# Products of the identity in gaps of TensorE: any free bank of PSUM in place of 128 columns at the end of the pair of banks

## The chip, the cores and the metric

One program runs on one core of a Trainium2 chip. The metric is device time in microseconds (us) of one execution, the median of three runs. Durations are read from one further execution that the hardware profiler recorded. Engines are named as the profile names them: PE is TensorE (matmuls) and PEld its weight loads, DVE is VectorE, ACT is ScalarE, POOL is GpSimd, SP is SyncE, which issues the DMAs.

## The reference

The reference is a two-layer diffusion backbone over 512 latent tokens and 256 context tokens of width 1024, all in float32. Each layer is a half-step SwiGLU, a token mixer and a second half-step SwiGLU, and each of them ends in a LayerNorm of `alpha * x + gate * f(x * (1 + scale) + shift)`, where gate, scale and shift come from a conditioning vector. The mixer of layer 0 is a bidirectional gated DeltaNet with four heads beside a Conformer module with a 31-tap depthwise convolution over 512 channels; that of layer 1 is grouped-query attention, eight query heads on two key heads, with normalised and rotated queries and keys.

```python
def ffn_sublayer(x, shift, scale, gate, w_gu, w_down, g, b):
    y = swiglu(modulate(x, shift, scale), w_gu, w_down)
    return deepnorm_residual(x, MACARON_WEIGHT * gate * y, g, b)

def even_mixer(...):    # layer 0: DeltaNet || Conformer, then one output projection
    o_l, _, _ = gdn_bidirectional(*lat_in, s_f, s_b)
    lat_out = merge(o_l, z_l, glu_l)
```

Nothing of this is computed by the instructions that the change touches.

## The kernel before

The kernel is first recorded and then ordered. `Program.record` notes every operation with the tiles that it reads and writes. `Program.order` then walks through a modelled time: whenever an engine is free, it takes the ready operation with the lowest rank that finds room for its tiles, and it writes one list of instructions for all engines. `Program.emit` turns this list into instructions, and semaphores between engines are set by the tile framework below it. So each engine runs its own queue strictly in the order that was planned, and all emitted instructions carry one line, 516 (517 in the changed kernel).

PSUM has eight banks of 512 float32 columns. Six of them are single places, tag `b`. The other two are one place, tag `bb`: one tile `pair` of 1024 columns, of which a tile of tag `bb` has the first 896. Only the convolution `conv31` asks for `bb`, for an accumulator of 783 columns that DVE updates tap by tap; when it is free, an ordinary tile of 512 columns may lie there too.

Where TensorE has nothing to do in the plan, `order` puts in a product of the identity with itself, 128x128, whose result nobody reads (lines 387 to 406). Each is a copy of one recorded matmul, `self.keep`; it stands in the list at the planned time, and none is added while enough of the planned time just before is work (`KEEP`). In the kernel before all of them write into columns 896 to 1023 of `pair`, one tile for the whole program, whatever else lies in the pair. A float32 matmul shows as two rows in the trace, so one product of the identity is two rows `pair<-ident`.

```python
if t.tag == "bb" or t is self.keep.tiles[0]:
    if pair is None:
        pair = p.tile([128, 1024], F32, name="pair")
    t.made = pair[:, 0:t.shape[1]] if t.tag else pair[:, 896:1024]
    continue
```

A tile with a tag gets a slot (`t.slot`), and `p.tile(..., tag=f"{tag}_{slot}", bufs=1)` makes it anew in that slot. Its first writer then waits for every instruction that used the tile which had the slot before; this is how a matmul that begins a new accumulation waits for the copy out of the old one.

Of the kernel before, what the change touches and what calls it, by code (L numbers as in the profile page):

```python
# [10 lines left out]
F32 = mybir.dt.float32  # L11
# [18 lines left out]
class View:  # L30
# [30 lines left out]
    def real(self):  # L61
        v = self.tile.made
        for f, a, k in self.how:
            v = getattr(v, f)(*a, **k)
        return v
# [26 lines left out]


CLASSES = {"p2": 512, "p4": 1024, "p6": 1536}
BANKS = {"b": 512, "bb": 896}


class Op:
# [19 lines left out]
class Program:  # L118
# [113 lines left out]
    def classes(self, occ):  # L232

        used = [t for t in self.tiles if t.tag and t.first is not None]
        for t in used:
            t.epoch = None
            if t.tag not in CLASSES:
                occ[t.tag][t.first:t.last + 1] += 1
            if t.tag in BANKS:
                t.places = [(c, None, n > BANKS[t.tag]) for c, n in BANKS.items() if n >= BANKS[t.tag] and self.slots[c]]  # L240
        ends = [b for b, _, _ in self.epochs[1:]] + [len(self.ops)]
# [23 lines left out]
    def order(self, look=40.0, reserve=1, ahead=40.0):  # L265
        ops = self.ops
        N = len(ops) - (self.keep is not None)
        if self.keep:
            ops.pop()
            self.keep.n = self.keep.deps[0]  # L270
            for t in self.keep.tiles:
                t.left -= 1
        users = [[] for _ in range(N)]
        for o in ops:
            o.wait, o.est, o.start = len(o.deps), 0.0, None
# [8 lines left out]
        occ, free = {}, {}  # L284
# [23 lines left out]
        wire, table, frontier, done = 0.0, 0, 0, 0  # L308
# [4 lines left out]
        now = 0.0  # L313
# [6 lines left out]
        def place(t, sync):  # L320

            for c, e, _ in sorted(t.places, key=lambda x: (x[2] > 0, x[0] != t.tag)) if t.places else ((t.tag, None, 0),):
                if e is not None and (e < self.now or any(left[:e])) or not free[c] or free[c][0][0] > now:
                    continue
                a = min(frontier, t.first)
                keep = reserve if sync and t.pool == "work" and t.places else 0
                if c != t.tag:
                    if occ[c][a:t.last + 1].max() + keep >= self.slots[c]:
                        continue
                elif t.first != frontier and a < t.first and occ[c][a:t.first].max() + keep >= self.slots[c]:  # L330
                    continue
                return c, e
            return None
# [11 lines left out]
        while done < N:  # L345
            moved = False
            for e in engines:
# [8 lines left out]
                while r and tries < 100:  # L356
                    c = heapq.heappop(r)
                    o = ops[c[1]]
# [23 lines left out]
                if pick is None and frontier < N:  # L382
                    o = ops[frontier]
                    if o.eng == e and not o.wait and o.est <= now and fits(o):
                        pick = (o.pri, o.n)
                if pick is None:
                    if e == "tensor" and self.keep and ops[self.keep.n].start is not None and ops[self.keep.n].end < now and 0 < frontier:
                        recent = [x for x in recent if x[1] > now - self.WINDOW]
                        if sum(y - max(x, now - self.WINDOW) for x, y in recent) < KEEP * self.WINDOW:
                            moved = True  # L390
                            o = Op()
                            for x in Op.__slots__:
                                setattr(o, x, getattr(self.keep, x, None))
                            o.n, o.deps, o.tiles, o.bytes = len(ops), [], self.keep.tiles, 0
                            ops.append(o)
                            while now >= edge:
                                warm = busy > 0.75 * self.WINDOW or warm and busy > 0.33 * self.WINDOW
                                busy, edge = 0.0, edge + self.WINDOW
                            cost = o.cost * (1 if warm else 2)
                            busy += cost  # L400
                            o.start, o.at, o.end = now, len(seq), now + cost
                            seq.append(o)
                            idle[e] = o.end
                            recent.append((now, o.end))
                        else:
                            again = now + 0.1
                    continue
                o = ops[pick[1]]
# [8 lines left out]
                for t in o.tiles:  # L417
                    if t.tag and t.slot is None:
                        c, e2 = place(t, o.eng == "sync")
# [59 lines left out]
            if not moved:  # L479
# [7 lines left out]
                now = min(nxt)  # L487
# [4 lines left out]
    def emit(self, tc, pools, seq):  # L492
        nc = tc.nc
        real = lambda v: v.real() if isinstance(v, View) else v
        self.names = {}
        now = part = pair = None
        with tc.manual_schedule():
            for o in seq:
                for t in o.tiles:
                    if t.made is None:  # L500
                        k = {"tag": f"{t.tag}_{t.slot}", "bufs": 1} if t.tag else {}
                        p = pools[t.pool]
                        if t.tag == "bb" or t is self.keep.tiles[0]:
                            if pair is None:
                                pair = p.tile([128, 1024], F32, name="pair")
                            t.made = pair[:, 0:t.shape[1]] if t.tag else pair[:, 896:1024]
                            continue
                        if t.epoch is not None:
                            if now != t.epoch:
                                if now is not None:  # L510
                                    part.release()
                                now, part = t.epoch, tc.alloc_tile_pool(name=f"part{t.epoch}", bufs=1, reuse_waits="tile")
                            p = part
                        t.made = p.tile(t.shape, t.dt, name=t.name, **k)
                f = getattr(getattr(nc, o.eng), o.f)
                i = f(*[real(x) for x in o.a], **{k: real(x) for k, x in o.k.items()})  # L516
                self.names[o.n] = i.ins.name
            if now is not None:
                part.release()
# [145 lines left out]
class Net:  # L665
# [7 lines left out]
        return self.nc.tile([128, 512], F32, "b", "psum", "b")  # L673

    def banks(self):
        return self.nc.tile([128, 896], F32, "bb", "psum", "bb")

    def page(self, dt=F32):
        return self.nc.tile([128, 1024], dt, "p4", "work", "p4")
# [1491 lines left out]
```

## Time and profile before

| | |
|---|---|
| median of 3 runs | 2856.68 us (2853.25 to 2857.43) |
| the profiled execution | 2857.14 us |
| its span in the trace | 2855.4 us |
| PE busy | 2811.3 us, 98% of the span |
| products of the identity | 748 rows, 103.4 us busy |
| granted TensorE clock, mean | 0.992 of 2.4 GHz |

The span runs from the first instruction of the program to the last, and the execution's own time is 1.74 us longer. A busy time is the union of the rows of an engine. Matmuls overlap in their pipeline, so two rows of 0.28 us that start 0.11 us apart take 0.11 us each from the engine's time. The granted clock has two levels here, 1.00 (2.4 GHz) and 0.50 (1.2 GHz).

### The profile page before, as it was taken

The page shows a single profiled execution, that of the slowest core. Times are in us where ns is not written, and L with a number is a line of the kernel's source. Part 1 is how long each engine was busy: PE and PEld are TensorE (multiplying, and loading weights), DVE is VectorE, ACT ScalarE, POOL GpSimd, SP SyncE. Part 2 cuts the span into 40 slices and gives each one's busy share as a digit, 9 for nine tenths or more (in the row PEclk, how much of TensorE's full clock was granted, in tenths as well). Part 3 has the DMA queues.
Part 4 walks back from the last instruction along what each step waited for, and adds up shares of the span by engine and source line. Part 5 has one row for each costly group of instructions (what it writes and reads, how often), then busy time and mean ns, then how long its engine had stood idle before and what let it go on. Part 6 is the DMA issues. An engine that isn't in the chain of part 4 may idle for free. (4 is left out here: it accounts for less than half of the span.)

```text
span 2855.4 us, 48739 instructions
## 1 busy us (share of the span) xinstructions
PE 2811.3 (98%) x19533; PEld 2675.8 (94%) x19533; DVE 2059.9 (72%) x3510; ACT 1136.8 (40%) x1990; POOL 475.4 (17%) x582
## 2 busy tenths in 40 slices
PE   9999999999999899999999999999999999999999
PEld 7999999988778899999999999999999887899998
DVE  3687777677968887787867678766656767788854
ACT  4343332154334744434322145443223555455522
POOL 3000000042865704000000030000003432200001
PEclk9999999999999999999999999999999999999999
DMA  7443465234631132343465225444621221144541
GB/s 243 132 141 115 140 210 181 83 97 137 162 91 44 53 114 88 117 131 124 133 201 188 82 82 170 128 131 155 218 80 31 78 70 48 47 135 143 173 120 46
DMA packets 386016, 346.98 MB, mean 122 GB/s; under 512 B 38528, under 2 KB 338813, under 8 KB 385789
## 3 DMA queue, kind: packets, MB, share of 16 engines
q1 hardware_dynamic: 385789, 343.86, 38.6%
q8 instruction: 154, 2.52, 0.4%
q14 instruction: 73, 0.60, 0.1%
HBM read 296.33 MB, written 47.48 MB: 120 GB/s over the span
## 5 line engine op out<-in xcount | busy, mean ns | idle before, releaser
L516 PE MATMUL b<-p,p 128*128 128x384 f32 (+4 forms) x15711 | 2463.3, 316 | 14.1 <-DVE p L516 6.6
L516 PEld LDWEIGHTS b<-p,p 128*128 128x128 f32 (+1 forms) x15711 | 2341.3, 189 | 86.9 <-issue 17.3
L516 ACT ACTIVATE p<-p 128x1024 fp32r<-128x1024 f32 (+9 forms) x871 | 696.3, 824 | 1093.8 <-PE b L516 410.6
L516 DVE TENSOR_TENSOR p<-p,p 128x1024 fp32r<-128x1024 f32 (+7 forms) x922 | 850.9, 943 | 263.4 <-PE b L516 135.7
L516 ACT ACTIVATE p<-b 128x384 f32<-128x384 f32 (+8 forms) x556 | 250.0, 464 | 485.6 <-PE b L516 445.5
L516 DVE TENSOR_TENSOR p<-p,b 128x384 f32<-128x384 f32 (+3 forms) x396 | 222.5, 578 | 99.0 <-PE b L516 64.0
L516 DVE SCALAR_TENSOR_TENSOR p<-b,gate,p 128x256 f32<-128x256 f32 (+1 forms) x415 | 167.5, 434 | 159.9 <-PE b L516 157.4
L516 POOL TENSOR_TENSOR p<-p,p 128x1024 fp32r<-128x1024 f32 (+18 forms) x157 | 139.1, 888 | 844.7 <-PE b L516 466.3
L516 POOL TENSOR_SCALAR p<-p,cA,cB 128x256 f32<-128x256 f32 x56 | 35.9, 645 | 1241.1 <-DVE p L516 1178.1
L516 DVE SCALAR_TENSOR_TENSOR p<-p,cond,p 128x1024 f32<-128x1024 f32 x161 | 203.0, 1278 | 9.9 <-DMA p<-in_ada_w_dram 9.8
L516 DVE SCALAR_TENSOR_TENSOR pair<-p,dw,pair 128x783 f32<-128x783 f32 x116 | 120.2, 1036 | 6.1 <-PE pair L516 3.4
L516 PE MATMUL pair<-ident 128*128 128x128 f32 x748 | 103.4, 284 | 9.2 <-DVE pair L516 3.7
L516 ACT ACTIVATE p<-p,cB,cA 128x256 f32<-128x256 f32 (+1 forms) x168 | 84.3, 589 | 65.4 <-DVE p L516 65.4
L516 PEld LDWEIGHTS pair<-ident 128*128 128x128 f32 x748 | 93.6, 196 | 16.2 <-ACT p L516 4.7
L516 POOL TENSOR_SCALAR p<-p,lnag 128x256 f32<-128x256 f32 x112 | 96.3, 869 | 3.2 <-DVE p L516 2.9
L516 DVE TENSOR_TENSOR p<-b,p 128x128 f32<-128x128 f32 (+4 forms) x168 | 70.0, 451 | 36.1 <-ACT p L516 18.9
L516 PE MATMUL pair<-p,p 128*128 128x256 f32 (+3 forms) x505 | 90.5, 314 | 0.1
L516 PE MATMUL b<-ident,p 128*128 128x128 f32 (+2 forms) x495 | 78.1, 282 | 3.4 <-DVE p L516 1.2
L516 PEld LDWEIGHTS pair<-p,p 128*128 128x128 f32 x505 | 75.8, 188 | 5.0 <-issue 1.4
L516 DVE TENSOR_TENSOR p<-p 128x512 f32<-128x512 f32 (+1 forms) x90 | 59.9, 674 | 26.0 <-PE b L516 18.5
L516 PEld LDWEIGHTS b<-ident,p 128*128 128x128 f32 (+2 forms) x495 | 59.4, 151 | 20.5 <-issue 7.8
L516 DVE SCALAR_TENSOR_TENSOR p<-p,p 128x384 f32<-128x384 f32 (+2 forms) x104 | 54.3, 534 | 9.2 <-ACT p L516 8.5
(162 smaller groups left out, 1152.8 us busy)
## 6 DMA issues: line engine op xcount, KB each, us to landing
p<-in_ffn_w_gu_dram SPq DMA_DIRECT2D x176, 512.0 KB
p<-in_ada_w_dram SPq DMA_DIRECT2D x144, 512.0 KB
p<-in_ffn_w_down_dram SPq DMA_DIRECT2D x96, 384.0 KB
hd<-p SPq DMA_DIRECT2D x54, 384.0 KB
p<-hd SPq DMA_DIRECT2D x27, 768.0 KB
p<-in_even_w_in_dram SPq DMA_DIRECT2D x25, 512.0 KB
xd<-p SPq DMA_DIRECT2D x24, 512.0 KB
p<-xd SPq DMA_DIRECT2D x24, 512.0 KB
```

The costliest lines, as they stand in the source:

```text
L516: i = f(*[real(x) for x in o.a], **{k: real(x) for k, x in o.k.items()})
```

## The change

The tile `bb` becomes the whole pair. A product of the identity now takes, at its planned time, a free place, `bb` first and then one of the `b`; it makes a new tile in that slot and gives the slot back at once. Where no place is free in the plan, no product is put in. The shared columns 896 to 1023 are gone.

```diff
-BANKS = {"b": 512, "bb": 896}
+BANKS = {"b": 512, "bb": 1024}
...
             for t in self.keep.tiles:
                 t.left -= 1
+            self.keep.tiles = self.keep.tiles[1:]
...
                 if pick is None:
-                    if e == "tensor" and self.keep and ops[self.keep.n].start is not None and ops[self.keep.n].end < now and 0 < frontier:
+                    place1 = next((c for c in ("bb", "b") if free[c] and free[c][0][0] < now), None) if e == "tensor" and self.keep else None
+                    if place1 and ops[self.keep.n].start is not None and ops[self.keep.n].end < now:
...
-                            o.n, o.deps, o.tiles, o.bytes = len(ops), [], self.keep.tiles, 0
+                            v = self.tile([128, 512], F32, "b", "psum", place1)
+                            v.tile.slot = heapq.heappop(free[place1])[1]
+                            o.n, o.deps, o.tiles, o.bytes = len(ops), [], [v.tile] + self.keep.tiles, 0
+                            o.a = (v[:, 0:128],) + self.keep.a[1:]
                             ops.append(o)
...
                             recent.append((now, o.end))
+                            heapq.heappush(free[place1], (now, v.tile.slot))
...
-                        if t.tag == "bb" or t is self.keep.tiles[0]:
-                            if pair is None:
-                                pair = p.tile([128, 1024], F32, name="pair")
-                            t.made = pair[:, 0:t.shape[1]] if t.tag else pair[:, 896:1024]
-                            continue
...
-        return self.nc.tile([128, 896], F32, "bb", "psum", "bb")
+        return self.nc.tile([128, 1024], F32, "bb", "psum", "bb")
```

The order of the instructions shows what comes of it. There are 374 products before and 243 after; the 17346 other matmuls are the same, and 13654 of them stand at the same place among themselves. What stands in brackets names the engine whose semaphore the instruction waits for.

The first place is PE's queue in the projections of layer 0, before the first matmul of the gates (`b_771`). It was:

```order
L516 MATMUL pair_88<-p6_662_5407,p4_806_5648 128x512
L516 MATMUL pair_88<-p6_666_5440,p4_806_5648 128x512
L516 MATMUL pair_88<-p6_662_5407,p4_807_5771 128x512
L516 MATMUL pair_88<-ident_2_70 128x128 [waits Activation_49]
L516 MATMUL pair_88<-ident_2_70 128x128 x28
L516 MATMUL b_771_6133<-gt_766_6128,cum0_749_5141 128x24 [waits DVE_49,Pool_49]
L516 MATMUL pair_88<-ident_2_70 128x128 x3
```

There are as many products now, each a new tile; these are the last of the 29 and the work behind them:

```order
L517 MATMUL b_3937_6196<-ident_2_70 128x128 [waits PE_49]
L517 MATMUL b_3938_6201<-ident_2_70 128x128 [waits PE_49]
L517 MATMUL b_3939_6203<-ident_2_70 128x128 [waits PE_49]
L517 MATMUL b_771_6206<-gt_766_6199,cum0_749_5164 128x24 [waits DVE_49,Pool_49]
L517 MATMUL b_3940_6208<-ident_2_70 128x128 [waits PE_49]
L517 MATMUL b_3941_6214<-ident_2_70 128x128 [waits PE_49]
L517 MATMUL b_3942_6216<-ident_2_70 128x128 [waits PE_49]
L517 MATMUL b_771_6206<-gt_766_6199,cum1_750_5196 128x24 [waits DVE_49,Pool_49]
```

Each product but the first now waits for PE's own semaphore, at the value that the product in the row above it sets; before, none of the 28 waited.

The second place is the end of PE's queue, behind the last matmul of the last layer (`b_3847`). It was:

```order
L516 MATMUL b_3847_28194<-p4_3822_28138,p4_3809_27682 128x512
L516 MATMUL b_3847_28194<-p4_3821_28130,p4_3810_27696 128x512
L516 MATMUL pair_88<-ident_2_70 128x128 x11
L516 MATMUL pair_88<-ident_2_70 128x128 [waits Activation_49]
L516 MATMUL pair_88<-ident_2_70 128x128 x44
L2165 UNCONDITIONAL_BRANCH
```

Of the 55 products that stand there now, these are the 10th to the 16th:

```order
L517 MATMUL b_4048_28362<-ident_2_70 128x128 [waits PE_49]
L517 MATMUL b_4049_28366<-ident_2_70 128x128 [waits PE_49]
L517 MATMUL b_4050_28370<-ident_2_70 128x128 [waits Activation_49]
L517 MATMUL b_4051_28373<-ident_2_70 128x128 [waits PE_49]
L517 MATMUL b_4052_28378<-ident_2_70 128x128 [waits PE_49]
L517 MATMUL b_4053_28381<-ident_2_70 128x128 [waits PE_49]
L517 MATMUL b_4054_28385<-ident_2_70 128x128 [waits PE_49]
```

The first eleven go round five banks, each waiting for the one five rows above or for ACT's copy; the twelfth waits for ACT's copy out of the pair, as before; the 43 behind it all use the pair, each waiting for the one above.

The third place is attention, where PE stood before with:

```order
L516 MATMUL pair_88<-ident_2_70 128x128 [waits DVE_49]
L516 MATMUL pair_88<-ident_2_70 128x128 x9
L516 MATMUL b_2883_21612<-p4_2761_21343,p4_2825_21374 128x256 [waits DVE_49,PE_49,Activation_49]
L516 MATMUL b_2883_21612<-p4_2762_21353,p4_2825_21374 128x256
L516 MATMUL b_2883_21612<-p4_2761_21343,p4_2826_21392 128x256
L516 MATMUL pair_88<-ident_2_70 128x128 x2
```

and has now:

```order
L517 MATMUL b_2878_21699<-p4_2874_21385,p6_2684_20769 128x256
L517 MATMUL b_2883_21758<-p4_2761_21498,p4_2825_21529 128x256 [waits DVE_49,PE_49,Activation_49]
L517 MATMUL b_2883_21758<-p4_2762_21508,p4_2825_21529 128x256
L517 MATMUL b_2883_21758<-p4_2761_21498,p4_2826_21547 128x256
L517 MATMUL b_2882_21766<-ident_2_70,p4_2880_21744 128x128 [waits DVE_49,Activation_49]
```

No place in PSUM is free in the plan there, and all 67 products of this stage are gone.

## Rows read from the trace of the kernel before

**Rows 1.** The page: span, busy time and instructions of each engine, granted clock in 40 slices.
```profile
span 2855.4 us, 48739 instructions
PE 2811.3 (98%) x19533; PEld 2675.8 (94%) x19533; DVE 2059.9 (72%) x3510; ACT 1136.8 (40%) x1990; POOL 475.4 (17%) x582
...
PEclk9999999999999999999999999999999999999999
```
**Rows 2.** The page's groups: out<-in, form, xcount | busy us, mean ns | idle before, releaser.
```profile
L516 PE MATMUL pair<-ident 128*128 128x128 f32 x748 | 103.4, 284 | 9.2 <-DVE pair L516 3.7
```
**Rows 3.** Timeline of PE from 650 us: start, duration, instructions [idle before <-releaser].
```profile
651.01 6.74 PE L516 MATMUL pair<-ident 128*128 128x128 f32 x58 [0.69 <-ACT p L516]
657.59 0.30 PE L516 MATMUL b<-gt,cum 128*128 128x24 f32 x2
657.73 0.91 PE L516 MATMUL pair<-ident 128*128 128x128 f32 x6
658.48 0.30 PE L516 MATMUL b<-gt,cum 128*128 128x24 f32 x2
```
**Rows 4.** Timeline of all engines at the end of the program.
```profile
2838.78 0.19 ACT L516 ACTIVATION_READ_ACCUMULATOR p<-pair 128x1 f32 x1
...
2839.03 10.31 PE L516 MATMUL pair<-ident 128*128 128x128 f32 x90 [0.78 <-ACT p L516]
...
2850.63 1.21 DVE L516 TENSOR_TENSOR p<-p,p 128x1024 f32<-128x1024 f32 x1
```
**Rows 5.** Timeline of PE: products at the cold start, and one alone at 951 us.
```profile
1.64 2.08 PE L516 MATMUL pair<-ident 128*128 128x128 f32 x8 [1.64 <-POOL ident L516]
...
3.86 1.22 PE L516 MATMUL pair<-ident 128*128 128x128 f32 x4
...
951.32 0.49 PE L516 MATMUL pair<-ident 128*128 128x128 f32 x2 [1.13 <-DVE pair L516]
```
**Rows 6.** Stretches of PE: length, busy (x rows), granted clock, DMA share, GB/s.
```profile
819.50:822.28 2.78, 0.25 (x2) 1.00 0.30 50
822.28:829.10 6.82, 6.82 (x22) 0.50 0.77 145
...
944.60:951.98 7.38, 4.93 (x41) 1.00 0.00 0
951.98:955.39 3.41, 3.41 (x25) 0.50 0.43 149
...
2250.00:2470.00 220.00, 212.68 (x1454) 1.00 0.21 63
```
**Rows 7.** Timeline of PE: two more long runs, and what follows them.
```profile
23.79 3.96 PE L516 MATMUL pair<-ident 128*128 128x128 f32 x34
27.55 0.74 PE L516 MATMUL b<-p,p 128*128 128x256 f32 x4
...
31.04 0.59 PE L516 MATMUL b<-p,cond 128*32 128x256 f32 x2 [1.25 <-DMA p<-in_ada_w_dram]
...
1107.54 5.40 PE L516 MATMUL pair<-ident 128*128 128x128 f32 x46
1113.64 0.74 PE L516 MATMUL b<-p,p 128*128 128x256 f32 x4 [0.71 <-ACT p L516]
```
**Rows 8.** Waits of PE: who waited for whom, us in total, times, longest.
```profile
PE pair L516 <- DVE pair L516: 3.7, 4, 1.3
```
**Rows 9.** Instructions on the tile pair: the taps, duration in ns min/median/max.
```profile
L516 DVE SCALAR_TENSOR_TENSOR pair<-p,dw,pair x116: 1023/1039/1041, 695.0 to 972.7; 128x783 f32<-128x783 f32 x116
```
**Rows 10.** Timeline of PE before the last stage's matmuls.
```profile
2819.60 3.07 PE L516 MATMUL pair<-ident 128*128 128x128 f32 x26
...
2822.77 1.67 PE L516 MATMUL b<-p,p 128*128 128x512 f32 x6
```

More of the change, by code (lines that the diff above doesn't have):

```diff
@@ L495, in emit @@
         self.names = {}
-        now = part = pair = None
+        now = part = None
         with tc.manual_schedule():
```

## Prediction

> **What bounds the kernel now.** I read the page first. PE is busy 98% of the span and idles 44 us in all [rows 1], so the kernel is bound by PE's queue: what delays the queue delays the end, save where one of these few idles can swallow it. The granted clock is near 1.00 in every slice, so PE also works at full speed. Then I read the groups: the products of the identity are 748 rows, 374 products, and take 103 us of PE [rows 2]. They lie where the plan has nothing else. The timelines of PE show how well they fit: the run of 29 from 651.01 us ends as the gap ends, and the matmul of the gates follows at once at 657.59 [rows 3]; likewise the runs from 23.79 and 1107.54 [rows 7]. A run that grew longer would push the work behind it. The last view is the end of the program: PE's last 45 products run from 2839.03 to 2849.34, while DVE's last instruction ends at 2851.84 [rows 4]. There PE is the earlier of the two by 2.5 us, and the span ends at 2855.4.
>
> **What a product costs before.** 90 rows take 10.31 us [rows 4], and one product alone takes 0.49 us from its start to its end [rows 5]. So each of the other 44 adds (10.31 - 0.49) / 44 = 0.223 us: they overlap in the pipeline, because none waits for another. At the cold start two products take 1.22 us and four 2.08 [rows 5]: 0.43 us for one more, 1.22 - 0.43 = 0.79 for one alone.
>
> **What a product costs after.** Every product is a new tile in a slot whose last user was most often the product just before it. I counted in the order: of 243 products 224 wait for PE's own semaphore, and 197 of these wait for the product directly ahead. No product before did so. A waiting product can't overlap: it starts after the other's end. No row shows an instruction of PE that waits for the one just ahead, so the price is bounded. From below it is 0.223 us, if the semaphore were seen at issue. From above it is the length of one alone and the step from a releaser's end to PE's start, which is 2838.97 to 2839.03, or 0.06 us [rows 4]: 0.49 + 0.06 = 0.55 us. I take the upper end, since that is how PE stands behind any other engine. At the low clock it is 0.79 + 0.06 = 0.85 us. So a waiting product costs 0.33 us more, and 0.63 us more where the clock has fallen.
>
> **Does the clock fall?** Between 944.60 and 951.98 PE runs products that stand apart by waits; the granted clock is 1.00 there and 0.50 in the 3.41 us behind it. An empty stretch of 2.8 us to 822.28 is followed by 6.8 us at 0.50 [rows 6]. Runs of waiting products look like the first of these: short idles between products, for longer. I take it that a run keeps the high clock for about as long as that stretch did, 7.2 us or 13 products, and then goes on at 0.85 us each.
>
> The Trainium skill, "TensorE: Matmul & The Clock Gate", section "A second HAM failure mode: psum-queue depth-cycling", says that a PE which goes round its PSUM banks and idles a little between groups makes its clock drop and return, and pays for it between the bursts. The trace agrees at the one place just told. With this rule the sum below is 67 us, without it 40 us.
>
> **The sum, against the profiled execution's 2857.1 us** (its span is 1.7 us shorter; it stands 0.4 us above the median of the runs).
>
> Long runs. With 13 products at 0.55, the others at 0.85 and the last at 0.43 before the next matmul can start:
> - 17 products at 23.79: 7.15 + 3 x 0.85 + 0.43 = 10.1 us where the gap was 3.76 [rows 7], so 6.4 more; of this the wait for a DMA at 31.04 can hide 1.25 [rows 7]. Left: +5.1.
> - 29 at 651.01: 7.15 + 15 x 0.85 + 0.43 = 20.3 against 6.58 [rows 3]: +13.7. Behind it stands the gates' chain through DVE, which nothing overlaps.
> - 24 at 1107.54 (23 before): 16.1 against 6.10 [rows 7]: +10.0.
> - The end: ACT's copy releases the pair at 2838.97 as before, then 44 products take 7.15 + 30 x 0.85 + 0.79 = 33.4, to 2872.5. The program's closing costs from 0 to 3.6 us (the latter is 2851.84 to 2855.4, with the last transfer in it); without a transfer I take 0.7. So 2873.2 for 2855.4: +17.8. What was hidden behind DVE by 2.5 us is then the last thing that ends.
>
> The four are 46.6 us; at the high clock throughout they are 4.0 + 9.0 + 6.8 + 8.5 = 28.3.
>
> Short runs. 197 - (16 + 28 + 23 + 43) = 87 waiting products are left; 6 lie ahead of the first transfers and 22 around 930 us. 59 x 0.33 = +19.5. Their gaps are full as well, as in [rows 3] at 657.73, where the next matmul follows in the row behind.
>
> The end of the DeltaNet stage, 927 to 955 us: 35 products at 0.223 and 3.7 us of waits for DVE's taps, which hold the pair [rows 8], give way to 25 products at 0.55 that wait for no tap: 13.8 - 11.5 = +2.3. The taps themselves gain nothing from a bank of their own, they take 1023 to 1041 ns whatever runs beside them [rows 9].
>
> Products that go. In attention 67 x 0.223 = 15 us of PE, in a stretch of which PE is busy 212.7 of 220 us [rows 6]. Where a product held work that was ready this is a gain, where PE would have waited it is none: 0 to -15; I take -6, since in my reading of that timeline PE still idles behind nearly half of the runs. Elsewhere 19 more go: 0 to -4, take -2. Where they leave PE empty the clock may fall, at 3.4 to 6.8 us of half speed [rows 6], or 1.7 to 3.4 us each: two such falls, +4. At 2819.60 thirteen products go and PE is empty for 3.2 us until 2822.77 [rows 10], longer than before the fall at 822.28: +2.5.
>
> After each of the three long runs within the program the clock stays low for at least 3.4 us of full work [rows 6]: 3 x 1.7 = +5.
>
> Together 46.6 + 19.5 + 2.3 - 6 - 2 + 4 + 2.5 + 5 = 72. Of PE's 44 idle us in the span some lie behind these places and wait for something that is not delayed; I take 5 off: **+67, so 2924 us**.
>
> **Rivals.**
> - The clock holds. For it: rows 6 have a single fall after spaced products, and that stretch held waits of up to 1.13 us [rows 5], longer than the 0.33 here. Then 28.3 + 19.5 + 2.3 - 6 - 2 + 2.5 - 5 = 40: 2897 us. The section of the skill named above speaks against it.
> - The runs inside are swallowed, and only the end counts: if the work behind a gap is later than the trace makes it look, because the stage's end hangs on DVE or POOL. For it: DVE is busy 72% [rows 1], and conv taps and scan run beside PE. Against it: the matmuls behind the long runs follow within 0.71 us [rows 3, 7]. Then +8.5 to +17.8, about 2870 us.
> - Faster: PE doesn't really wait for itself, since a matmul's semaphore would be up by the time the next is issued. Then a product costs 0.223 us as before, there are 131 fewer, and the 3.7 us of waits for the taps [rows 8] go too: -6 - 2 - 4 = -12, 2845 us. It decides below about 0.25 us from product to product. Against it: the pipeline overlaps rows of 0.28 us [rows 2], and the end of a row, not its start, is what has released every waiter in these views.
>
> **How the numbers follow.** The fall of the clock 0.62; the clock holds 0.24; only the end 0.08; faster 0.06, of which a third could shrink into no change. A measurement of this kernel can tell 0.2%, 5.7 us, from no change. So slower 0.94, same 0.02, faster 0.04. The likeliest case alone, with 0.55 to 0.9 us at the low clock and none or 15 us of gain in attention, reaches from 2905 to 2950; with the case of the held clock and its own spread the range is 2880 to 2950, and what lies outside it is the last two cases and the tails of the first, 2 in 10.
>
> **What would show it.** Products in the run from 651 us about 0.55 us apart, later 0.85, and the matmul of the gates some 14 us later behind it; the granted clock at 0.50 inside that run and inside the one before the end; PE's last product ending behind DVE's last instruction, by 10 to 20 us; fewer products' rows than before, about 486, but more PE time per product. It is wrong if products stand 0.22 us apart, if the span ends with DVE as before, or if the gates start as early after 651 us as they did.

## The result, and the profile after

The changed kernel takes 2900.09 us (2895.02 to 2902.49) where the kernel before takes 2856.68: a ratio of 1.0152, 95% interval 1.0127 to 1.0177, slower by 43 us. Its profiled execution is 2895.02 us long, 37.9 us more than that of before. The forecast was 2924, and the rival "the clock holds" 2897.

The page of the changed kernel, against [rows 1]:

```profile
span 2893.1 us, 48210 instructions
PE 2837.3 (98%) x19271; PEld 2660.3 (92%) x19271; DVE 2059.0 (71%) x3510; ACT 1135.5 (39%) x1988; POOL 478.7 (17%) x582
...
PEclk9999999899999999999999999999999999999999
```

PE is busy 26.0 us longer with 262 rows fewer, and idles 55.8 us in place of 44.1. The other engines do what they did. PEclk falls below 0.9 nowhere but in one slice, from 506 to 579 us.

The group of the products, against [rows 2]:

```profile
L517 PE MATMUL b<-ident 128*128 128x128 f32 x486 | 116.6, 326 | 14.9 <-POOL ident L517 1.6 <-ACT p L517 0.9 <-DVE p L517 0.8
```

There are 243 products for 374, and yet 116.6 us for 103.4. The long runs in PE's timeline (start, duration, instructions), against [rows 3] and [rows 7]:

```profile
21.47 9.13 PE L517 MATMUL b<-ident 128*128 128x128 f32 x34
30.36 0.72 PE L517 MATMUL b<-p,p 128*128 128x256 f32 x4
...
657.40 15.79 PE L517 MATMUL b<-ident 128*128 128x128 f32 x58 [0.69 <-ACT p L517]
673.03 0.30 PE L517 MATMUL b<-gt,cum 128*128 128x24 f32 x2
673.25 1.58 PE L517 MATMUL b<-ident 128*128 128x128 f32 x6
674.67 0.30 PE L517 MATMUL b<-gt,cum 128*128 128x24 f32 x2
...
1128.47 13.06 PE L517 MATMUL b<-ident 128*128 128x128 f32 x48
1141.29 0.72 PE L517 MATMUL b<-p,p 128*128 128x256 f32 x4
```

The same 29 products take 15.63 us from the first to the matmul of the gates, where they took 6.58; the next matmul still follows at once. The granted clock inside this run, by stretches (length, PE busy, PEld busy, DVE, ACT, POOL, clock, DMA share, GB/s):

```profile
657.40:660.80 3.40, 3.05 (x13) 1.90 (x14) 3.40 (x9) 1.03 (x3) 0.00 (x0) 1.00 0.00 0
...
667.60:671.00 3.40, 3.05 (x14) 1.78 (x12) 0.00 (x0) 0.00 (x0) 0.00 (x0) 1.00 0.00 0
```

It is 1.00 from end to end, where the forecast had 0.50 from the 14th product on. So it is in the run of 24 and in the one behind the last matmul (length, PE busy, clock, DMA share, GB/s):

```profile
1128.47:1141.29 12.82, 11.48 (x52) 1.00 0.63 205
2866.00:2892.34 26.34, 23.83 (x111) 1.00 0.20 80
```

Here the forecast failed. The end of the program, all engines, against [rows 4]; the weight loads show the spacing of the products:

```profile
2880.78 1.21 DVE L517 TENSOR_TENSOR p<-p,p 128x1024 f32<-128x1024 f32 x1
...
2891.31 0.30 PEld L517 LDWEIGHTS b<-ident 128*128 128x128 f32 x2 [0.25 <-PE b L517]
2891.85 0.30 PEld L517 LDWEIGHTS b<-ident 128*128 128x128 f32 x2 [0.25 <-PE b L517]
```

```profile
2866.00 26.34 PE L517 MATMUL b<-ident 128*128 128x128 f32 x110
```

Each product of these rows is released by PE itself (`<-PE b`), 0.547 us after the one before. DVE is done at 2881.99, PE at 2892.34: the last thing that ends is now a product whose result nobody reads.

**Where the 37.7 us of span lie.** I matched the matmuls that both traces have and took the difference of their starts, as a median over 25 us of the time before:

| time before, us | shift at the end of it | what changed in it |
|---|---|---|
| to 200 | -0.3 | -2.3 ahead of the run of 17, +2.0 behind it, given back between 100 and 200 |
| 550 to 575 | +4.1 | +4.4: a fall of the clock that before did not have |
| 600 to 650 | +6.4 | +2.3: the run of 8 products |
| 650 to 675 | +15.8 | +9.4: the run of 29 |
| 925 to 975 | +13.2 | +0.6 between 675 and 925, then -3.2: 927 to 955 us |
| 1000 to 1125 | +27.1 | +13.9: runs of 11, 9 and 24 |
| to 2850 | +30.2 | +3.1: all the rest, attention among it |
| the end | +37.7 | +7.5: PE's last product behind DVE |

### The profile page after: what moved, and what is told of

It reads as the page before. It is cut to its first block, busy times and chain, and to the rows that moved or that the text cites. A ratio compares the mean times of both kernels' runs of the same rounds, so it can differ in the third digit from the quotient of the medians.

```text
span 2893.1 us, 48210 instructions
## 1 busy us (share of the span) xinstructions
PE 2837.3 (98%) x19271; PEld 2660.3 (92%) x19271; DVE 2059.0 (71%) x3510; ACT 1135.5 (39%) x1988; POOL 478.7 (17%) x582
## 5 line engine op out<-in xcount | busy, mean ns | idle before, releaser
L517 PE MATMUL b<-p,p 128*128 128x384 f32 (+4 forms) x16216 | 2539.9, 316 | 21.4 <-DVE p L517 11.8
L517 PEld LDWEIGHTS b<-p,p 128*128 128x128 f32 (+1 forms) x16216 | 2414.5, 189 | 105.1 <-issue 24.1
L517 ACT ACTIVATE p<-b 128x384 f32<-128x384 f32 (+9 forms) x576 | 258.7, 465 | 492.1 <-PE b L517 445.7
L517 PE MATMUL b<-ident 128*128 128x128 f32 x486 | 116.6, 326 | 14.9 <-POOL ident L517 1.6
L517 PEld LDWEIGHTS b<-ident 128*128 128x128 f32 x486 | 73.5, 192 | 56.9 <-PE b L517 50.9
L517 DVE SCALAR_TENSOR_TENSOR bb<-p,dw,bb 128x783 f32<-128x783 f32 x116 | 120.1, 1036 | 2.7
L517 DVE TENSOR_TENSOR p<-b,p 128x128 f32<-128x128 f32 (+4 forms) x184 | 77.0, 452 | 44.9 <-ACT p L517 24.9
L517 PEld LDWEIGHTS b<-ones,p 128*128 128x128 f32 x368 | 58.6, 203 | 0.3 <-PE b L517 0.3
L517 DVE SCALAR_TENSOR_TENSOR p<-p,qw,p 128x772 f32<-128x772 f32 x48 | 57.6, 1212 | 0.1
```

## The experiments

None of these kernels leaves out anything that is read. In e3_none and e5_later the plan also puts some of the other work in another order; in all others the products are all that differs. Ratios are to the kernel before in the same session, with 95% intervals.

**e1_share: take away the wait alone.** The changed kernel with the same 243 products in the same order, but a product that follows a product in the same place uses its tile again.

```diff
-                            v = self.tile([128, 512], F32, "b", "psum", place1)
-                            v.tile.slot = heapq.heappop(free[place1])[1]
+                            slot = heapq.heappop(free[place1])[1]
+                            if (place1, slot) not in mine:
+                                mine[place1, slot] = self.tile([128, 512], F32, "b", "psum", place1)
+                            v = mine[place1, slot]
+                            v.tile.slot = slot
```

> The changed kernel with its 243 products at the same places of the same order; only, a product that comes into a place which a product had last writes into that product's tile and makes none of its own, so it does not wait for it. Theory (the price is the wait of a product for the one before): a run of 29 from about 650 us takes 6.5 us again in place of 15.6, the end of the program is DVE's, and the 9.4 us gained by the gates, 9.0 at 1107 us, 3.6 at 1057 us, 2.4 at 620 us and 7.5 at the end go away: about 2857 to 2862 us, with the loss at 550 us (13 products become 2, some 4 us) still there. Rival (the price is where and how many the products are: fewer of them, in other banks, and the work reordered with them): stays at 2890 to 2900 us.

2864.12 us, 1.0027 [1.0016, 1.0037]. Its group of products:

```profile
L522 PE MATMUL b<-ident 128*128 128x128 f32 x486 | 63.6, 284 | 3.4 <-POOL ident L522 1.6 <-ACT p L522 0.9 <-DVE p L522 0.8
```

Busy time and idle before it fall from 116.6 + 14.9 to 63.6 + 3.4 us, by 64.5 us, or 0.327 us for each of the 197 waits on the product directly ahead. Of these 64.5 us 36 (2900.1 - 2864.1) reach the end. Of the others some lie beside waits that were there anyway: behind the last matmul 43 waits, 14 us, cost 7.5, since DVE ends in between. Some are lost again to the clock: in the profile of e1_share the clock is at 0.50 for 72 us, in that of the changed kernel for 48 (mean clock 0.987 and 0.992), and 24 us at half speed are worth at most 12. How the rest divides was not measured. The wait of PE for itself is the price, which is shown: nothing else differs between the two orders. The 7.5 us (2864.1 - 2856.6) by which e1_share is still above the kernel before belong to the fewer products and the new order of the work; of these only the fall at 550 us was tried by itself (e9_no550).

**e2_notail: take away the end.** The changed kernel without the 55 products behind the last matmul.

```diff
-                    if place1 and ops[self.keep.n].start is not None and ops[self.keep.n].end < now:
+                    if place1 and any(o.start is None for o in mms) and ops[self.keep.n].start is not None and ops[self.keep.n].end < now:
```

> The changed kernel without the 55 products behind the last matmul of the layers. Theory: the span ends with DVE's last instruction and the transfer behind it again, 7.5 us earlier: about 2892 us where the changed kernel has 2900. Rival (the end of the program hangs on DVE and the transfer also in the changed kernel): no change.

2892.28 us, 1.0130 [1.0108, 1.0151]: 7.8 us less by the medians, though the two intervals overlap. The trace is clearer: DVE is the last again, and its end at 2883.59 is 3.6 us ahead of the span's, as before.

**e3_none: what the products are worth.** The kernel before with no products (`KEEP = 0.0` for 0.7).

> The kernel before without any product of the identity. It tells what the products give: gaps of 2.5 us and more (about ten) are each followed by 3.4 to 6.8 us at half the clock, 1.7 to 3.4 us lost each, against some 15 us in which products held work that was ready or waited for the taps. Theory: 2860 to 2880 us, so less than the changed kernel, whose products cost more than they give. Rival (without products PE goes cold again and again): over 2900 us.

2860.21 us, 1.0010 [1.0000, 1.0021]. The mean clock is 0.978 in place of 0.992, and the kernel is some 3.6 us slower, in an interval that begins at no difference. Since some of the other work stands in another order as well, the 3.6 us are not the products' alone. The kernel without any is some 40 us faster than the changed one.

**e4_half: shorter products.** The changed kernel with products of 64 columns.

```diff
-                            o.a = (v[:, 0:128],) + self.keep.a[1:]
+                            o.a = (v[:, 0:64], self.keep.a[1], self.keep.a[2][:, 0:64])
```

> The changed kernel with products of 64 columns in place of 128, so that PE streams half as long in each and still waits as often. If the clock holds in the runs of the changed kernel because PE streams for enough of the time, it now falls to 0.50 inside the run from 657 us and inside the one at the end, and the work behind goes on at half speed for 3.4 to 6.8 us each: 2885 to 2905 us, with products about 0.44 us apart before the fall. If short idles between products do not lower it whatever the products are, it stays at 1.00 there and each waiting product is cheaper by about 0.1 us: 197 x 0.1 = 20 us less, 2880 us.

2937.4 us, 1.0279 [1.0258, 1.0299]: slower than with 128 columns, by 37 us, and beyond both of the times expected. Stretches of the run of 29 and of the end:

```profile
662.25:666.30 4.05, 3.59 (x17) 2.49 (x17) 4.00 (x9) 0.86 (x3) 0.00 (x0) 0.99 0.02 4
666.30:681.80 15.50, 14.35 (x44) 10.59 (x44) 1.46 (x4) 4.20 (x6) 0.00 (x0) 0.50 0.00 0
2894.30:2898.56 4.26, 4.09 (x31) 3.54 (x29) 4.23 (x15) 1.99 (x7) 1.93 (x1) 1.00 0.01 2
2898.56:2928.40 29.84, 27.55 (x81) 20.05 (x80) 11.44 (x27) 3.39 (x4) 5.07 (x2) 0.50 0.18 70
```

At the high clock the shorter products stand 0.492 us apart, not much closer than the long ones, and then, after some 4 us, both runs fall to 0.50 and stay there to their ends, 0.747 us apart. The run of 17 falls after 3.46 us, and that of 24 is at 0.50 from its start, behind a shorter run that fell. The forecast's picture is right for these, though with 4 us in place of 7.2: the run at the end falls though PE was busy for all of the 4.30 us ahead of it.

**e5_later: let the products go round the banks.** A product gives its slot back at its planned end in place of its start.

```diff
-                            heapq.heappush(free[place1], (now, v.tile.slot))
+                            heapq.heappush(free[place1], (o.end + self.LAT, v.tile.slot))
```

> The changed kernel, but a product gives its slot back in the plan at its planned end and not at its planned start, so that successive products go round the free banks: 217 products, of which 24 wait for the one directly ahead and 69 for the one two rows up. Theory (the price is the wait for the product directly ahead, 0.547 us from product to product in place of 0.22): two rows up the wait is nearly over when it is reached, 0.55 / 2 = 0.28 us a product; 24 x 0.33 + 69 x 0.06 = 12 us in place of 65, so 2864 (as with shared tiles) + 6 to 12 = 2868 to 2876. Rival (any new tile in a slot costs, whoever had it): as slow as the changed kernel, 2895 to 2903.

2869.5 us, 1.0041 [1.0029, 1.0054], within the theory's range and 5.4 us above e1_share. A new tile in a used slot costs little when the product that had it is two or more rows up; with 26 products fewer and some of the other work in another order, what it costs exactly can't be read from this.

**e6_one and e11_one: one run alone.** e1_share, with the 29 products ahead of the gates a new tile each.

```diff
-                            if (place1, slot) not in mine:
+                            made += 1
+                            if (place1, slot) not in mine or 60 < made <= 89:
```

> The kernel with shared tiles (same order and products as the changed kernel, no product waits for one), but the 29 products of the run that precedes the gates are again a new tile each: 28 waits for the product directly ahead, at this one place. Theory (this run delays the work behind it by its own growth and the clock holds in it): 28 x (0.547 - 0.223) = +9.1 us, 2873 for 2864.1. Rival 1 (the delay is absorbed within the stage, as that of the 17 products at 24 us was): 2864 to 2867. Rival 2 (the clock falls in the run, as forecast): +14, 2878.

2873.37 us, 1.0057 [1.0037, 1.0077], 9.3 us over e1_share: the number of the theory, and yet not by its road. The timeline and the stretches of its profile:

```profile
652.11 23.35 PE L523 MATMUL b<-ident 128*128 128x128 f32 x58 [0.69 <-ACT p L523]
675.26 0.46 PE L523 MATMUL b<-gt,cum 128*128 128x24 f32 x2
```

```profile
651.02:654.44 3.42, 2.50 (x11) 1.33 (x10) 3.42 (x9) 1.62 (x4) 0.00 (x0) 1.00 0.00 0
654.44:678.34 23.90, 22.52 (x64) 14.61 (x64) 3.99 (x11) 4.20 (x6) 0.00 (x0) 0.50 0.00 1
```

In the fifth product the clock falls, and for 23.90 us it does not come back, although PE is busy 22.52 of them; the products stand 0.853 us apart. The matmuls behind the run are 18 us later than in e1_share, and 6 us of that are made good by the end, at places where e1_share's profile has falls of its own. So was the first profile of the changed kernel just luck? Both kernels once more, unaltered:

> The changed kernel once more, unaltered, for a second profile and more times. In its first profile the granted clock was 1.00 in all its long runs; the same 29 products fell to 0.50 after four of them in the profile of the kernel in which they alone wait. Theory (the fall inside such a run differs from execution to execution of the same program): one or more of the runs of 29, 24, 17 or 55 is at 0.50 in this profile, and where it is, products stand 0.853 us apart; times from 2893 to 2910, median 2896 to 2904. Rival (the first profile shows what this kernel always does): 1.00 in all four again, and times within some 4 us of 2897.

> The kernel in which the run of 29 alone waits for itself, once more, unaltered, for a second profile and more times. Theory (the fall differs from execution to execution): this time the run may stay at 1.00, 0.547 us apart, with the gates 9 us later than with shared tiles instead of 18; the median time over more runs lies between the two, 2870 to 2877. Rival (this program always falls there): 0.50 from the fourth or fifth product on again, 0.853 us apart.

Both profiles show what the rivals said. The changed kernel: 2900.2 us (2898.2 to 2905.1), 1.0156 [1.0140, 1.0171], and 1.00 again in all its long runs; here that of 29 and the end:

```profile
657.41:673.03 15.62, 14.01 (x59) 1.00 0.01 1
2869.21:2895.40 26.19, 23.72 (x111) 1.00 0.20 80
```

The kernel with one run: 2879.6 us, 1.0079 [1.0064, 1.0094], which is 14.9 us over e1_share by the ratios where the first time it was 8.6, and the fall again, one product later, for 23.89 us:

```profile
652.36:655.78 3.42, 2.61 (x11) 1.66 (x12) 3.12 (x9) 1.38 (x4) 0.00 (x0) 1.00 0.00 0
655.78:679.67 23.89, 22.57 (x67) 14.67 (x69) 3.34 (x11) 4.20 (x6) 0.00 (x0) 0.50 0.00 1
```

Two profiles of each program agree. That is too few to say that it belongs to the program whether the run falls: other falls come and go between two profiles of the same program. The changed kernel has them at 798 and 843 us in its first profile and not in its second, which has others at 880, 2423 and 2467 us.

**e12_two and e13_late: what makes this run fall.** e12_two lets the eight products at 620 us wait for themselves too (`52 < made <= 89`); e13_late lets only the last 22 of the 29 wait (`67 < made <= 89`).

> The kernel in which the run of 29 alone waits for itself (the granted clock fell after four of the 29 in both its profiles), with the run of 8 products at 620 us waiting for itself as well, as in the changed kernel. The 29 are the same, with the same empty stretch ahead of them, but begin some 2.3 us later, at about 654.5 us. Theory (it decides where in the execution the empty stretch and the first products fall: in the changed kernel the run began at 657.4 us and held): 1.00 throughout the 29, 0.547 us apart; the two runs add 2.3 + 9.1 us to the 2864 with shared tiles: about 2875, less than the 2878 measured without the second run (median of both batches). Rival (the fall belongs to a run of waiting products behind this gap, and the changed kernel escapes it by something else): 0.50 from the fourth or fifth product, 2880 or more.

> The same kernel, with the first seven of the 29 products sharing a tile (0.22 us apart) and only the other 22 waiting for the one ahead. Theory (a run of waiting products does not make the clock fall by itself; the empty 0.7 to 1.1 us ahead of it together with the idles between the first products did): 1.00 throughout, 22 x 0.324 = 7.1 us more than with shared tiles, about 2871. Rival (waiting products lose the clock anyway, as forecast): 0.50 within the 22, 0.853 us apart: 2877 to 2880.

2874.69 us, 1.0066 [1.0049, 1.0083], and 2869.97 us, 1.0055 [1.0040, 1.0070]: 11.2 and 8.0 us over e1_share by the ratios (1.0027), where 11.4 and 7.1 were expected. The run in e12_two, timeline and stretches:

```profile
658.09 15.77 PE L523 MATMUL b<-ident 128*128 128x128 f32 x58 [0.69 <-ACT p L523]
673.70 0.30 PE L523 MATMUL b<-gt,cum 128*128 128x24 f32 x2
```

```profile
658.09:661.50 3.41, 3.06 (x13) 1.92 (x14) 3.41 (x9) 1.03 (x3) 0.00 (x0) 1.00 0.00 0
661.50:673.60 12.10, 10.84 (x46) 6.63 (x47) 2.54 (x6) 4.20 (x6) 0.00 (x0) 1.00 0.00 1
```

And in e13_late:

```profile
654.89 13.84 PE L523 MATMUL b<-ident 128*128 128x128 f32 x58 [0.69 <-ACT p L523]
668.57 0.30 PE L523 MATMUL b<-gt,cum 128*128 128x24 f32 x2
```

```profile
658.30:668.50 10.20, 9.11 (x39) 5.61 (x39) 2.11 (x6) 4.20 (x6) 0.00 (x0) 1.00 0.00 0
```

Both hold at 1.00. In e12_two the products, the gap ahead of them and what follows are those of e6_one; the run of eight ahead is slower, and the start is another, 658.09 for 652.11 (654.5 was expected). So a run of 128-column products that wait for each other does not lose the clock by itself, and not by the 0.69 us gap ahead of it either. The empty stretch together with the first idles may tip it, at some moments and not at others; no run here shows that. e13_late's denser start cannot be told from its place: it too began later, by 2.8 us. Whether the place in the program or the chance of an execution decides, one profile of e12_two and two of e6_one's kernel can't tell. Why the run falls in these stays open.

**e9_no550: a fall where products are missing.** The kernel before without the 13 products at 548 to 553 us (these are passed over when the list is turned into instructions).

> Before, without the 13 products (9 and 4) that stand between 548 and 553 us; the other 361 and the order of the rest are unchanged. Theory (the changed kernel lost 4.4 us there because, with no free place in the plan, these 13 became 2, PE stood empty for some 2 us and the granted clock fell to 0.50 for 10 us behind it): the clock falls there, +3 to +5 us, 2860 to 2862. Rival (that fall comes from somewhere else, or moves to where it does no harm): within 1 us of before.

2862.3 us, 1.0015 [1.0005, 1.0026]. Its stretches, and those of the changed kernel, which has 2 of the 13:

```profile
549.72:559.96 10.24, 9.52 (x44) 9.52 (x45) 4.19 (x5) 0.00 (x0) 0.00 (x0) 0.50 0.02 5
```

```profile
545.00:552.74 7.74, 6.43 (x43) 5.82 (x42) 7.73 (x9) 1.06 (x1) 0.00 (x0) 1.00 0.00 0
552.74:562.98 10.24, 10.24 (x51) 10.24 (x50) 3.61 (x5) 0.00 (x0) 0.00 (x0) 0.50 0.00 0
```

The fall comes with the missing products, 10.24 us in both, and the matmuls behind it are 4.1 us later here, 4.4 there. This part of the change is shown alone. A shorter fall, 3.41 us, stands near that place in e8_hybrid below, which has all 13 products.

**e8_hybrid: the idea without its price.** The kernel before, where only the products that find the pair held in the plan, by the convolution or by another tile, go to a free bank and share a tile there. In the trace 48 move: 27 between 928 and 947 us, but also six at 549, three near 1008 and twelve at 2836.

```diff
+                            if not (free["bb"] and free["bb"][0][0] < now) and free["b"] and free["b"][0][0] < now:
+                                took = heapq.heappop(free["b"])[1]
+                                if took not in mine:
+                                    mine[took] = self.tile([128, 512], F32, "b", "psum", "b")
```

> Before, with one difference: where the convolution's tile holds the pair in the plan, the products take a free bank of the six instead, all products of one stay there sharing one tile; elsewhere they stay in the columns at the end of the pair. No product waits for a product, and 46 of the 374 move. Theory (it is the wait for PE itself that made the change slow, and a bank other than the pair is right where the pair is held): the 3.7 us of waits for the taps between 927 and 955 us go, and the fall of the clock at 952 us may go with them: 2850 to 2854, 3 to 6 us under before. Rival (the end of the DeltaNet stage hangs on DVE's taps and not on PE there): within 2 us of before.

2857.15 us, 1.0001 [0.9989, 1.0013]: the rival. The profile has the matmuls at 950 us 2.8 us earlier relative to those ahead, and the fall at 952 us [rows 6] is gone, but others are 1.9 us late at 550 us, where six products moved, and 1.4 us at 750, where none did. The theory was only half tried, since four products behind 948 us stayed in the pair and 2.0 of the 3.7 us of waits for the taps with them:

```profile
948.72 0.94 PE L530 MATMUL pair<-ident 128*128 128x128 f32 x6 [0.86 <-DVE pair L530]
950.78 0.49 PE L530 MATMUL pair<-ident 128*128 128x128 f32 x2 [1.13 <-DVE pair L530]
```

Whether a microsecond or two is gained can't be told from this. No version here beats the kernel before.

## Why the prediction was right or wrong

- **The time**: 2900 lies in the range of 2880 to 2950 because the range took in the rival "the clock holds", 2897. The likeliest case, 2905 to 2950 by its own spread, did not come. The rival's mechanism is what the runs show; that its sum is so near is in part luck, since terms told below miss in both directions.
- **PE's queue bounds the kernel, and full gaps don't hide a longer run**: right at 620 and 650 us and between 1000 and 1125, where the matmuls behind the runs moved with them; not for the run of 17.
- **The price of a wait**: right at both clocks. 0.55 us was taken and 0.547 measured; 0.85 at the low clock, and 0.853 in e6_one. At 0.547 us a product starts only when the one ahead, 0.49 us long, has ended, so the faster rival had nothing to stand on.
- **"I take it that a run keeps the high clock for about as long as that stretch did, 7.2 us or 13 products, and then goes on at 0.85 us each"**: this is the step that failed. It read the length of the one such stretch of [rows 6] as the time that any run of waiting products has. In two profiles of the changed kernel no long run fell, 43 products in a row at the end among them; in e6_one the run fell in its fifth product, in e11_one in its sixth. What makes a run fall stays open. The waits of up to 1.13 us in the stretch of [rows 6] are no answer: e8_hybrid still has one of 0.86 and one of 1.13 us there, and its clock holds. The four long runs, set at 46.6 us (28.3 with the clock held), measured 9.1 (29 products; 15.63 us for 6.58), 6.7 (24; 12.82 us for 6.10), 7.5 (the end) and 4.3 (17), together 27.6; the +5 for the clock behind them had nothing to pay for. These two terms are 24 us, of the 29 between the forecast and the profiled execution to which its sum was worked out.
- **The rule of the Trainium skill** ("TensorE: Matmul & The Clock Gate", section "A second HAM failure mode: psum-queue depth-cycling"), which the forecast followed, has a PE that idles a little between groups lose its clock and get it back. With 64 columns the traces of e4_half agree with the loss, and all four long runs stand at 0.50; the clock did not come back within them. With 128 columns and products that wait the long runs agree with it only in e6_one and e11_one.
- **Short runs**: set at +19.5. The shifts show +2.3 (620 us) and +7.2 (1000 to 1125 us, the 13.9 less the 6.7 of the run of 24); the rest is not found as a shift.
- **The run of 17**: of 5.1 us that should stay (4.0 with the clock held), 4.3 were there right behind it, from -2.3 to +2.0 us, and none at 200 us. The kernel now has 21 products between 31 and 620 us where it had 42, which would give some of it back; no run isolated this.
- **927 to 955 us**: +2.3 was forecast, -3.2 came. That PE no longer waits for taps was counted; the fall at 952 us, which is gone too, was not, but its 3.41 us at half speed are worth no more than 1.7. The rest stays open.
- **Products that go**: attention and the rest were set at -4, with +4 for falls and +2.5 for the gap at 2819.60. Attention and all behind 1125 us came to +3.1, of which 1.6 near 2825 us, at a fall of 3.41 us. That fewer products would let the clock fall was foreseen, without a place; at 550 us one such fall cost 4.4 us alone, more than the two falls of the sum.
- **The end**: the mechanism was right, PE's last product replaces DVE. 0.7 us was taken for the closing, and 2893.1 - 2892.3 is 0.8.

## What to carry to other kernels

Look in the order, not in the diff, for a wait of an engine on itself: a new tile in a slot that the instruction just ahead used turns a pipelined 0.223 us into 0.547 us, here for work that nobody reads. Where such fillers must change place, let them share a tile or go round the banks (e1_share, e5_later: 31 to 36 us of the 43 back), and put none behind the last real matmul. A fall of the clock seen once beside a pattern is no rule for the pattern: find a second place that has the pattern without the fall before it goes into the sum.

## What the runs showed that was not expected

- The same 29 matmuls, 0.547 us apart and behind the same gap, kept the granted clock at 1.00 in three profiles, where they began at 657.4 us (twice) and 658.1, and dropped to 0.50 after four or five in two, where they began at 652.1 and 652.9. Whether the start decides is not shown. Once low they stayed low to their end, 23.9 us, with PE busy 94% of that time.
- Halving the columns of a waiting product saves only 0.055 us of its 0.547, and the granted clock is at 0.50 in all four long runs.
- 374 products, 103 us of PE, are worth some 3.6 us, 0.10% [0.00, 0.21], with some of the other work in another order; 13 of them that were missing cost 0.15% [0.05, 0.26].
